# Hybrid decoder trunk: the forget sums' transfer to DRAM is issued by ScalarE's queue instead of SP's

## The chip, the core and the metric

The kernel runs on one core of a Trainium2 chip. A core has five engines, each with its own queue of instructions: TensorE (PE, with its weight loads as PEld), VectorE (DVE), ScalarE (ACT), GpSimd (POOL) and SyncE (SP), which computes nothing and issues transfers. They wait for each other through semaphores. The metric is the device time of one execution in microseconds; of several runs the median is taken.

## What is computed

Two layers of a decoder trunk over 528 tokens (16 learned meta tokens and 512 real ones) of width 1024, in float32. In each layer a normalised input goes through one input projection; half of its columns feed eight heads of forgetting attention, half feed four heads of retention; their outputs go through one output projection and are added; then a SwiGLU feed-forward with 2816 hidden columns follows. At the end the tokens are normalised and the meta tokens are dropped.

The part that the change touches is the decay of the forgetting attention. Eight columns of the projection are forget gates, one per head:

```
logf = log_sigmoid(flog + b_fgate)
c    = cumsum(logf, axis=1)
s    = q k^T * scale + c[t] - c[s],  s <= t
p    = softmax(s)
```

The running sum c is needed along the keys, that is, as one row of 528 numbers per head which every query's partition must see. Within a row of the softmax, c[t] is a constant and falls out, so that the kernel only uses the part over the keys.

## The kernel before

All activations lie transposed, channels on the 128 partitions and the 528 tokens along the row. Every float32 product is made of three products of split numbers: a high part (a cast) and a low part (the difference), for weights and activations; so a weight tile of 128x1024 is loaded by SP into one of three `raw` buffers (`fetch`, L158), cast in two halves by ScalarE into `whi` (L191), subtracted by GpSimd or VectorE into `wlo` (L194), and then used by TensorE (L217). The load of a tile waits in SP's queue until an earlier tile's splitting has set its buffer free.

The order of TensorE's work is written out by hand: `layer` builds lists of steps (projections, attention heads, retention heads) and merges them by places, so that the steps of the heads stand between those of the projections. The order on the other engines is made by a scheduler that takes the instructions' priorities and dependences; only the instructions that are pinned keep the program's order. A transfer stands in the queue of the engine that issues it, at the place which the scheduler gives it there, and a queue is worked off in order.

The piece around the change, once per layer:

- `forget_gates` (L367) multiplies the normalised input by the gates' weights and leaves the eight gates as rows of 528 in `z`.
- `forget_sums` (L389) scales them, takes the log-sigmoid with ScalarE (L394 to L396) and VectorE (L397, L398), and sums along the row by a scan (L399). The result, 8 partitions by 528, 16.5 KB, is written to a tensor in DRAM, `cdr` (L401).
- `scores` (L492) of each head reads its row of `cdr` back into all 128 partitions, a tile `bc` of 264 KB, two buffers (L497, issued by SP). Then for each block of queries TensorE makes the scores (L507), VectorE adds the mask (L513) and subtracts `bc` while taking the row's minimum (L514), and ScalarE takes the exponential (L527).

```
        nc.vector.tensor_tensor_scan(z2, z, z, 0.0, ALU.add, ALU.max)
        st["cdr"] = tc.dram_tile([FH, T], F32, name=f"cdr{l}")
        nc.sync.dma_start(st["cdr"], z2)
...
                nc.sync.dma_start(bc, ly["cdr"][hd:hd + 1, :].partition_broadcast(128))
```

Other names that are used below: `kh` and `kl` are the split keys of the head pair (L451, L452), `vt` the transposed values (L458 and L627), `vv` the split values after TensorE's transposes (L418, L483, L484). PSUM tiles are `psa` (four buffers, scores and transposes) and `psd` (two buffers, projections): a step that needs a `psa` buffer waits until the reader of its last use is done.

Of the kernel before, what the change touches and what calls it, by code (L numbers as in the profile page):

```python
# [39 lines left out]
def hybrid_kernel(ctx, tc, x_t, w_in, w_fl, w_out, w_gate, w_up, w_down, vecs, b_fg, rope, decay, mask, ident, out_t):  # L40
    nc = tc.nc
# [224 lines left out]
    def tt(name, dt=F32):  # L266
        tag, bufs = tags[name]
        return tmp.tile([128, T], dt, name=name, tag=tag, bufs=bufs)
# [120 lines left out]
    def forget_sums(l, st):  # L389
        z = st["z"]  # L390
        z2 = tt("z2")[0:FH]
        with ExitStack() if l else tc.high_priority():
            nc.vector.scalar_tensor_tensor(z, z, RSC, st["R"][0:FH, :], ALU.mult, ALU.mult)
            nc.scalar.activation(z2, z, AF.Abs, bias=bfg[:, l:l + 1])  # L394
            nc.scalar.activation(z2, z2, AF.Exp, scale=-1.0)
            nc.scalar.activation(z2, z2, AF.Ln, bias=onec[0:FH])  # L396
        nc.vector.tensor_scalar(z, z, bfg[:, l:l + 1], 0.0, ALU.add, ALU.min)  # L397
        nc.vector.tensor_sub(z, z2, z)  # L398
        nc.vector.tensor_tensor_scan(z2, z, z, 0.0, ALU.add, ALU.max)  # L399
        st["cdr"] = tc.dram_tile([FH, T], F32, name=f"cdr{l}")  # L400
        nc.sync.dma_start(st["cdr"], z2)  # L401

    LOGS = "natural_log_exp_and_others"
    ROOTS = "abs_reciprocal_sqrt_and_small"
# [821 lines left out]
    def layer(l):  # L1226
# [62 lines left out]
        def first_parts():  # L1289
            ly["parts"] = col_parts(ly["acc"], FULL, True)  # L1290
            convert(3, NK, True)

        sums = [lambda: forget_sums(l, ly)]
        plan = [lambda: enter_att(l), start]
        if l == 0:
# [109 lines left out]
```

## Time and profile before

| what | value |
|---|---|
| time, median of 3 runs | 1274.46 us (1274.37 to 1275.15) |
| the profiled execution's own time | 1278.19 us |
| its span, first to last instruction | 1276.3 us |
| mean granted TensorE clock | 0.995 |
| busy share: PE, PEld, DVE, ACT, POOL | 99%, 94%, 78%, 54%, 21% |
| transfers by SP's queue (q1) | 118.77 MB, 29.8% of 16 engines' span |
| transfers by ScalarE's queue (q10) | 0.29 MB |
| cdr to DRAM, issued by SP | twice, at 36.0 and 672.0 us |

Times in the profile are microseconds from the span's start. The profile's rows give start and length, the engine, the line of the kernel, the operation, and the output and input tiles; a count follows the x. In brackets stand the engine's idle time just before the row and what ended it. SPq and ACTq mark what SP's and ScalarE's sequencers do themselves: issuing transfers and waiting. The chain of waits is followed back from the last instruction: at each step to what released it. A row of it that begins with DMA lasts from the issue to the moment at which the waiting engine went on.

### The profile page before, as it was taken

How to read it: one execution, taken by the hardware profiler on the slowest of the kernel's cores; microseconds unless marked ns; L12 is line 12 of the kernel's file. 1: busy time of each engine (PE TensorE's matmuls, PEld its weight loads, DVE VectorE, ACT ScalarE, POOL GpSimd, SP SyncE). 2: the span in 40 equal slices, each digit the busy share in tenths (PEclk: the TensorE clock that was granted, in tenths of full speed). 3: DMA queues.
4: the chain of work that ended last, by engine and by line, in shares of the span. 5: the costliest groups of instructions: out<-in, count | busy, mean ns of one | idle time of the engine just before them, and what ended most of it. 6: DMA issues, size and time to landing. Idle time of an engine off the chain costs nothing.

```text
span 1276.3 us, 23615 instructions
## 1 busy us (share of the span) xinstructions
PE 1258.8 (99%) x9271; PEld 1199.9 (94%) x9271; DVE 996.6 (78%) x1843; ACT 688.2 (54%) x1246; POOL 265.2 (21%) x522
## 2 busy tenths in 40 slices
PE   9999999999999999999999999999999999999997
PEld 8899999999999999999998989999789999999996
DVE  7777856779988887887785777567899888888866
ACT  6666545676444444444464665456764444444444
POOL 3355546420000000000025545554100000000000
PEclk9999999999999999999999999999999999999998
DMA  6322232223333333332323232232224333333321
GB/s 216 93 68 84 79 94 72 74 67 112 108 96 100 100 100 100 100 100 83 102 74 100 76 100 84 75 92 67 99 86 129 100 100 100 100 99 101 106 76 67
DMA packets 45680, 120.57 MB, mean 94 GB/s; under 512 B 5360, under 2 KB 12272, under 8 KB 45568
## 3 DMA queue, kind: packets, MB, share of 16 engines
q1 hardware_dynamic: 45136, 118.77, 29.8%
q8 instruction: 73, 1.20, 0.4%
q14 instruction: 39, 0.32, 0.1%
q10 hardware_dynamic: 432, 0.29, 0.1%
HBM read 116.91 MB, written 2.13 MB: 93 GB/s over the span
## 4 chain that ended last, share of the span: by engine, by line
PE 94%; DVE 2%; ACT 1%; DMA 1%; issue 0%; DVEq 0%; ACTq 0%; SPq 0%
PE psd L217 30%; PE psa L880 18%; PE psd L1015 14%; PE psd L880 13%; PE psa L217 5%; PE psa L1015 4%; PE psa L418 2%; PE psa L572 2%; PE psa L507 2%; PE psa L729 1%; PE psa L699 1%; DMA bc<-cdr 1%; PE psa L379 1%; PE psa L290 0%; DMA cdr<-z 0%
## 5 line engine op out<-in xcount | busy, mean ns | idle before, releaser
L194 POOL TENSOR_TENSOR wlo<-raw,whi 128x128 fp32r<-128x128 f32 x504 | 259.9, 551 | 293.5 <-ACT whi L191 293.5
L217 PE MATMUL psd<-xh,whi 128*128 128x264 f32 (+1 forms) x792 | 197.1, 316 | 0.6 <-ACT whi L191 0.6
L217 PE MATMUL psd<-xh,wlo 128*128 128x264 f32 (+1 forms) x792 | 187.7, 305 | 0.0
L217 PE MATMUL psd<-xl,whi 128*128 128x264 f32 (+1 forms) x792 | 187.3, 304 | 0.4 <-DVE xl L320 0.4
L217 PEld LDWEIGHTS psd<-xh,whi 128*128 128x128 f32 x792 | 129.4, 191 | 5.7 <-ACT whi L191 1.3
L217 PEld LDWEIGHTS psd<-xh,wlo 128*128 128x128 f32 x792 | 128.0, 190 | 6.4 <-DVE wlo L194 0.4
L217 PEld LDWEIGHTS psd<-xl,whi 128*128 128x128 f32 x792 | 128.6, 190 | 4.8 <-DVE xl L320 0.8
L191 ACT CAST whi<-raw 128x512 fp32r<-128x512 f32 (+1 forms) x168 | 98.5, 614 | 51.6 <-PE psd L217 38.2
L868 ACT CAST whi<-raw 128x1024 fp32r<-128x1024 f32 (+2 forms) x62 | 54.9, 886 | 51.0 <-PE psd L880 39.5
L868 ACT CAST fwhi<-raw 128x1024 fp32r<-128x1024 f32 (+2 forms) x62 | 55.7, 898 | 46.6 <-PE psd L880 39.2
L1115 POOL TENSOR_TENSOR th<-th,e 128x544 f32<-128x544 f32 x1 | 1.4, 1370 | 359.1 <-DVE e L1135 359.1
L85 POOL MEMSET kl<- 64x528 f32 x2 | 1.1, 534 | 345.4 <-PE psa L880 345.4
L869 DVE TENSOR_TENSOR wlo<-raw,whi 128x1024 fp32r<-128x1024 f32 (+2 forms) x62 | 62.9, 1015 | 12.1 <-ACT whi L868 12.0
L869 DVE TENSOR_TENSOR fwlo<-raw,fwhi 128x1024 fp32r<-128x1024 f32 (+2 forms) x62 | 64.0, 1032 | 9.6 <-ACT fwhi L868 9.5
L880 PE MATMUL psa<-th,whi 128*128 128x264 f32 (+1 forms) x232 | 65.4, 282 | 0.0
L880 PE MATMUL psa<-th,wlo 128*128 128x264 f32 (+1 forms) x232 | 65.4, 282 | 0.0
L880 PE MATMUL psa<-tl,whi 128*128 128x264 f32 (+1 forms) x232 | 65.3, 282 | 0.0
L880 PE MATMUL psa<-th,fwhi 128*128 128x264 f32 (+1 forms) x224 | 63.4, 283 | 0.0
L880 PE MATMUL psa<-tl,fwhi 128*128 128x264 f32 (+1 forms) x224 | 63.3, 283 | 0.0
L880 PE MATMUL psa<-th,fwlo 128*128 128x264 f32 (+1 forms) x224 | 63.2, 282 | 0.0
L527 ACT ACTIVATE probs<-probs,nmax 128x144 f32<-128x144 f32 (+1 forms) x64 | 36.9, 577 | 47.3 <-DVE nmax L514 34.5
L868 ACT CAST fwhi<-S 128x1024 fp32r<-128x1024 f32 x20 | 21.0, 1050 | 69.1 <-PE psa L880 67.1
(340 smaller groups left out, 4053.7 us busy)
## 6 DMA issues: line engine op xcount, KB each, us to landing
raw<-w_in SPq DMA_DIRECT2D x54, 512.0 KB, 3.5
raw<-w_gate SPq DMA_DIRECT2D x44, 512.0 KB, 3.8
fraw<-w_up SPq DMA_DIRECT2D x38, 512.0 KB, 3.5
raw<-w_down SPq DMA_DIRECT2D x64, 256.0 KB, 2.8
raw<-w_out SPq DMA_DIRECT2D x16, 512.0 KB, 3.4
raw<-w_down SPq DMA_DIRECT2D x32, 192.0 KB, 2.5
bc<-cdr SPq DMA_DIRECT2D x16, 264.0 KB, 3.4
raw<-w_up SPq DMA_DIRECT2D x6, 512.0 KB, 3.6
```

Source lines behind the costliest of these rows:

```text
L191: pin(nc.scalar.copy(hi, job["raw"][:, c0:c1]), pinned)
L194: pin(sub(lo[:, i:i + step], job["raw"][:, c0 + i:c0 + i + step], hi[:, i:i + step].bitcast(F32)), pinned)
L217: nc.tensor.matmul(ps[1][b][:, 0:c1 - c0], w[:, wk, :], x[:, c0:c1], start=(k == 0 and i == 0), stop=(k == n - 1 and i == 2))
L379: nc.tensor.matmul(ps[:, 0:c1 - c0], wf[:, k, :], st["x"][k][part][:, c0:c1], start=(i == 0), stop=(i == 2 * NK - 1))
L418: nc.tensor.transpose(ps[:, 128 * j:128 * j + 128], src[:, o:o + 128], idt)
L507: nc.tensor.matmul(sc[0:nq, 0:c1 - c0], st["q"][s][:, q0:q0 + nq], kk[:, c0:c1], start=(i == 0), stop=(i == 1))
L527: nc.scalar.activation(pr, pr, AF.Exp, bias=nmax[0:nq], scale=-1.0, accum_out=rsum)
L572: nc.tensor.matmul(po[:, c0:SEQ], v[:, j, :], pp[:, j, META + c0:T], start=(j == 0 and i == 0), stop=(j == 4 and i == 1))
L868: nc.scalar.copy(hi, src)
L869: nc.vector.tensor_sub(lo, src, hi.bitcast(F32))
L880: nc.tensor.matmul(bank()[:, 0:b.shape[-1]], a[:, o + k, :], b, start=(fresh and k == 0 and i == 0), stop=(k == n - 1 and i == 2), skip_gr ...
L1015: nc.tensor.matmul(v[:, 0:c1 - c0], a[:, s * n + k, :], b[:, c0:c1], start=(k == 0 and i == 0), stop=(k == n - 1 and i == 2))
```

## The change

`forget_sums` hands its transfer to ScalarE's queue. Nothing else in the text of the kernel is touched.

```
         nc.vector.tensor_sub(z, z2, z)
         nc.vector.tensor_tensor_scan(z2, z, z, 0.0, ALU.add, ALU.max)
         st["cdr"] = tc.dram_tile([FH, T], F32, name=f"cdr{l}")
-        nc.sync.dma_start(st["cdr"], z2)
+        nc.scalar.dma_start(st["cdr"], z2)
```

What this does to the order of the queues, in layer 1 first. SP's queue after the loads of the angles (`cr`, `sr`), before the change:

```order
L1237 DMA cr<-rope 128x528
L1237 DMA sr<-rope 128x528
L158 DMA raw<-w_in 128x1024
L679 DMA dec<-decay 128x528
L158 DMA raw<-w_in 128x1024 x2
L401 DMA cdr_8605<-z_8597 8x528
L497 DMA bc<-cdr_8605 128x528 x2
L158 DMA raw<-w_in 128x1024 x2
```

Now the L401 is gone, and the two reads of `cdr` stand right behind the two weight loads. It stands in ScalarE's queue instead, which reads now, from the log-sigmoid to the first exponential of the attention:

```order
L394 ACTIVATE z_8597<-z,bfg 8x528
L395 ACTIVATE z_8597<-z_8597 8x528
L396 ACTIVATE z_8597<-z_8597,onec 8x528
L191 CAST whi<-raw 128x512 x2
L451 CAST kh_8672<-tq 64x528 x2
L401 DMA cdr_8605<-z_8597 8x528
L451 CAST kh_8676<-tq 64x528 x2
L191 CAST whi<-raw 128x512 x3
L527 ACTIVATE probs,sums<-probs,nmax 128x144
```

Before, the same rows stood there without the L401.

In layer 0 the transfer comes behind all four casts of the keys on ScalarE, and one cast of the values (`vv_603`) moves up ahead of the first exponentials:

```order
 L451 CAST kh_428<-tq 64x528 x2
 L451 CAST kh_432<-tq 64x528 x2
+L401 DMA cdr_424<-z_414 8x528
 L191 CAST whi<-raw 128x512 x2
 L483 CAST vv_602<-psa 128x4x64
 L483 CAST vv_602<-psa 128x64
+L483 CAST vv_603<-psa 128x4x64
 L527 ACTIVATE pm_113,rsum<-pm_113,nmax 16x16
 L527 ACTIVATE probs,sums<-probs,nmax 128x144
-L483 CAST vv_603<-psa 128x4x64
```

VectorE's order in layer 0 follows this: the first subtraction of the values (L484) now stands ahead of the first step that reads `bc` (L514).

```order
 L627 SCALAR_TENSOR_TENSOR vt_108<-psd,R 128x528
 L513 TENSOR_TENSOR psa<-psa,msk 128x128
+L484 TENSOR_TENSOR vv_602<-psa,vv_602 128x4x64
 L514 ISA pm_113,nmax<-psa,bc 16x16
 L514 ISA nmax 16x1
 L514 ISA probs,nmax<-psa,bc 128x144
 L514 ISA nmax 128x1
-L484 TENSOR_TENSOR vv_602<-psa,vv_602 128x4x64
```

Behind these rows five more subtractions, masks and L514 steps of the same blocks change places with each other. The order on TensorE and GpSimd is the same as before, and so is VectorE's in layer 1.

More of the change, by code (lines that the diff above doesn't have):

```diff
@@ L400, in forget_sums @@
         st["cdr"] = tc.dram_tile([FH, T], F32, name=f"cdr{l}")
-        nc.sync.dma_start(st["cdr"], z2)
+        nc.scalar.dma_start(st["cdr"], z2)
     LOGS = "natural_log_exp_and_others"
```

## The prediction

> **What bounds the kernel now.** I read the page first, then the waits of TensorE, then the chain of waits in layer 1, and last the timelines of the queues around it.
>
> ```profile
> span 1276.3 us, 23615 instructions
> PE 1258.8 (99%) x9271; PEld 1199.9 (94%) x9271; DVE 996.6 (78%) x1843; ACT 688.2 (54%) x1246; POOL 265.2 (21%) x522
> ```
>
> TensorE is the bound; a change pays only if it shortens one of its few stalls. These are the waits in which it took part near the two transfers that are moved (engine and line, what ended the wait, total, times, longest):
>
> ```profile
> PE psa L418 <- DVE vv L484: 1.8, 1, 1.8
> PE psa L507 <- DVE nmax L514: 1.1, 1, 1.1
> PE psa L418 <- DVE nmax L514: 0.6, 1, 0.6
> ```
>
> The 1.8 and the 0.6 stand in layer 1, the 1.1 in layer 0. What leads to those of layer 1 is told by the chain of waits from 660 to 690 us (start, length, what):
>
> ```profile
> 671.60 0.33 SPq L158
> ...
> 671.98 3.25 DMA cdr<-z
> ...
> 675.24 3.90 DMA bc<-cdr
> ...
> 679.28 0.31 DVE probs L514
> ...
> 683.42 0.41 PE psa L418
> ```
>
> The forget sums go to DRAM (cdr) and come back broadcast (bc), and the first scores step of the attention waits for bc. That round trip is on the path. Was it started as soon as it could be? The timelines of VectorE and SP, and a stage row (stretch, length, busy us of PE, PEld, DVE, ACT, POOL, the granted clock, DMA share, GB/s) answer:
>
> ```profile
> 666.25 1.40 DVE L399 TENSOR_TENSOR_SCAN z<-z 8x528 f32<-8x528 f32 x1
> 659.27 12.66 SPq L158 DMA_DIRECT2D raw<-w_in  x2
> 662.90:671.60 8.70, 8.70 (x75) 8.70 (x74) 5.68 (x9) 6.72 (x11) 5.52 (x9) 1.00 0.00 1
> ```
>
> The scan ends at 667.65. SP issues cdr only at 671.98, 4.33 us later: it stands in SP's queue behind a weight load that waits for its buffer until 671.60, while the DMA engines lie idle (share 0.00). And cdr then takes 3.25 us, since it travels behind 512 KB of weights.
>
> **What the change removes and adds.** Two issues leave SP and join ScalarE, one per layer; the bytes are the same. In layer 0 VectorE's and ScalarE's orders shift a little too.
>
> When does ScalarE issue? In its queue cdr stands behind casts (kh), and behind it stand the other casts. Whether the issue waits for the casts ahead to finish is shown by how far its sequencer runs ahead (instruction, count, ns min/median/max, first and last start; ACTq is the sequencer):
>
> ```profile
> L191 ACTq EVENT_SEMAPHORE  x1: 4291/4291/4291, 665.2 to 665.2; - x1
> 666.43 2.60 ACT L451 CAST kh<-tq 64x528 fp32r<-64x528 f32 x4
> L191 ACTq EVENT_SEMAPHORE  x1: 3550/3550/3550, 33.9 to 33.9; - x1
> 33.84 2.60 ACT L451 CAST kh<-tq 64x528 fp32r<-64x528 f32 x4 [0.47 <-DVE tq L444]
> ```
>
> The wait behind the four casts began at 665.2 and at 33.9, when the casts had hardly begun: the sequencer had handed them over. So cdr needs only the scan.
>
> *Layer 1, the round trip.* Issue at 667.68 (scan end 667.65 plus about 0.03). In layer 0, with nothing ahead in the queue, the same transfer took 1.47 (row below), so it is in DRAM at about 669.2. SP goes on being held until 671.60, issues its weight load (0.33), and then bc at 671.98, in cdr's old place, without a wait: 3.26 earlier than 675.24. When does bc land? It now rides directly behind 512 KB of weights, which before cdr did. Nearest rows: the pair took 3.90 in the chain above; a later bc, issued 0.43 after a weight load, landed 3.6 after its issue:
>
> ```profile
> 806.41 0.33 SPq L158 DMA_DIRECT2D raw<-w_in  x1
> 806.84 0.38 SPq L497 DMA_DIRECT2D bc<-cdr  x1
> DMA to landing us min/median/max: 3.6/3.6/3.6
> raw<-w_in SPq DMA_DIRECT2D x54, 512.0 KB, 3.5
> ```
>
> That is 675.6 to 675.9 against 679.15. I take 675.9. The bound on the other side is no overlap at all: the weights land 3.5 after 671.60 (their median, last row), then 3.90: 679.0.
>
> *Layer 1, TensorE.* Its rows around the stall, then the same work at full pace, and the granted clock:
>
> ```profile
> 679.85 0.34 PE L507 MATMUL psa<-kh,qs 128*128 128x400 f32 x1
> 680.03 0.34 PE L507 MATMUL psa<-kl,qs 128*128 128x400 f32 x1
> 680.96 0.66 PE L418 MATMUL psa<-idt,vt 128*128 128x128 f32 x4 [0.58 <-DVE nmax L514]
> 683.42 0.41 PE L418 MATMUL psa<-idt,vt 128*128 128x128 f32 x1 [1.80 <-DVE vv L484]
> ...
> 686.99 0.40 PE L217 MATMUL psd<-xh,whi 128*128 128x512 f32 x1
> 677.20 0.40 PE L217 MATMUL psd<-xh,whi 128*128 128x512 f32 x1
> 677.90 0.71 PE L418 MATMUL psa<-idt,vt 128*128 128x128 f32 x5
> 678.37 0.48 PE L217 MATMUL psd<-xh,whi 128*128 128x512 f32 x1
> 62.94 0.49 PE psa L507 x4
> 683.40:687.00 3.60, 3.58 (x12) 3.08 (x13) 3.01 (x11) 0.72 (x2) 0.00 (x0) 0.53 0.44 146
> ```
>
> TensorE could have gone on at 680.21 (680.03 plus the 0.18 from 679.85 to 680.03). From there to 686.99 it does five transposes, three psd matmuls, four L507 matmuls and three psd matmuls. At full pace that is 0.47 (677.90 to 678.37) + 0.70 (677.20 to 677.90) + 0.49 + 0.70 = 2.36, so 682.57. It took until 686.99: 4.42 us lost. From 683.42 to 686.99 alone one transpose (0.09) and 1.89 of matmuls took 3.57, so 1.59 of the loss is the clock, granted at 0.53 after the stalls. The other 2.83 is standing still.
>
> How early must bc be for the loss to vanish? Both stalls end a fixed chain after bc (679.15): the first at 680.96, 1.8 after it; the second at 683.42, 4.27 after it. TensorE comes to them at 680.21 and, four transposes later, at about 680.6. So bc must land by 678.4 for the first and by 676.3 for the second. 675.9 meets both, with 0.4 to spare on the second. Gain: **4.42**.
>
> The Trainium skill, "TensorE: Matmul & The Clock Gate" (Part 1: The HAM clock gate), says the clock falls to half after an idle window of about 3.4 us. Here it fell after 0.58 and 1.80 us of idling with transposes between, shorter than that window. By the rule alone the 1.59 would not be there and the sum would be 2.83; I go by the row.
>
> *Layer 1, what stands behind.* On ScalarE the last two kh casts start some 0.3 later (an issue holds the sequencer 0.33 on SP), at 668.0; the subtraction that reads them ends before 669.6, when VectorE waits 0.48 for TensorE:
>
> ```profile
> 669.62 0.77 DVE L458 SCALAR_TENSOR_TENSOR vt<-psa,R 128x264 f32<-128x264 f32 x2 [0.48 <-PE psa L217]
> ```
>
> So nothing; without that cover, 0.3 at most. SP's next weight load stood behind the bc pair and comes earlier by at most as much as bc; it rides behind bc, not ahead of it.
>
> *Layer 0.* Here SP was not held up (chain of waits, then VectorE and TensorE):
>
> ```profile
> 34.70 1.23 DVE L399 TENSOR_TENSOR_SCAN z<-z 8x528 f32<-8x528 f32 x1
> 35.96 1.47 DMA cdr<-z
> 37.45 3.84 DMA bc<-cdr
> 41.43 0.16 DVE L514 CUSTOM_DVE_ANT_0 pm<-psa,bc 16x16 f32<-16x16 f32 x1 [2.18 <-DMA bc<-cdr]
> 41.66 0.39 PE L507 MATMUL psa<-kh,qs 128*128 128x272 f32 x1 [1.09 <-DVE nmax L514]
> ```
>
> The scan ends at 35.93; from ScalarE's sequencer the issue is again at about 35.96. The next wait on ScalarE lasts to 37.4, which hides the issue itself. If the issue had to wait for the four casts (end 36.44), the round trip and TensorE's 1.09 would grow by 0.49. Bounds: 0 and 0.49 lost; no gain is possible, since cdr already left with the scan's end. I take 0, by the two sequencer rows. The subtraction L484 that now stands ahead of L514 on VectorE runs in the 2.18 that VectorE waits for bc, so the L514 that ends TensorE's wait does not move; if L484 came too late it would push L514 by its own length, well under that wait, and I take nothing for it.
>
> *Afterwards.* Does TensorE keep the 4.4?
>
> ```profile
> 700.00:1200.00 500.00, 499.61 (x3269) 454.96 (x3268) 399.14 (x701) 272.84 (x476) 105.04 (x208) 1.00 0.31 95
> ```
>
> From 700 to 1200 us it is busy 499.61 of 500, so work that comes earlier ends earlier. Sum: 1274.46 - 4.42 - 0 = **1270.0 us**. The profiled execution took 1278.19 with its span of 1276.3, 3.7 above the median of the runs; the difference of two executions is carried over to that median.
>
> **The rivals.**
>
> *The clock term is missing in unprofiled runs.* The stall stays, its aftermath doesn't, because the fall of the clock after so short a stall is chance: for it, the 1.09 in layer 0 left no half-clock stretch; against it, one row shows it. Then 1274.46 - 2.83 = 1271.6.
>
> *The queue of weights keeps bc.* cdr is early, but bc now waits behind the 512 KB itself and lands near 679.0: gain 0.15, so 1274.3. For it: cdr needed 3.25 there against 1.47. Against it: the 3.6 of the bc at 806.84. It decides from a landing after 678.4 (nothing left but part of the second stall). The Trainium skill, "DMA: Bandwidth & Descriptors" (Issuing engines are not separate DMA queues), says that a second issuing engine saves only the sequencer's issue time; that speaks for this rival. The idle 8.7 us show that here it is a wait, not an issue, that is spared.
>
> *Given back.* TensorE runs 4.4 ahead of the weights' splitting, and stalls on POOL's slow halves:
>
> ```profile
> 692.82 2.64 POOL L194 TENSOR_TENSOR wlo<-raw,whi 128x128 fp32r<-128x128 f32 x4 [2.10 <-ACT whi L191]
> ```
>
> These wait on ScalarE, which follows the round trip and moves by 3.26, about 1.2 less than TensorE. If that were all stall: 1271.2; with a second one of that kind or a fall of the clock, 1273.
>
> *Slower: ScalarE's own DMA queue is slow.* Its only earlier weights took 4.8 to land:
>
> ```profile
> raw<-w_in ACTq DMA_DIRECT2D x2, 128.0 KB, 4.8
> ```
>
> Were cdr to take 4.8, bc in layer 0 would start 3.3 later, TensorE would stand 4.4 and then run 1.59 longer at half clock: 4.9 lost, against 4.4 won in layer 1 (cdr landed at 672.5, bc 2.8 earlier): 1275.0. From 4.3 on the change loses. Against it: those loads went out beside all of the start's traffic, cdr alone.
>
> That ScalarE's issue waits for casts would not undo the change: 0.49, so 1270.5. That is inside the forecast.
>
> **How the numbers follow.** Forecast 62%, the missing clock term 13%, weights keep bc 11%, given back 7%, slow queue 7%. 0.2% is 2.55 us, about what the runs can tell apart. Faster by more: 62, 10 of the 13 (1271.6 lies 0.3 inside the bound) and 3 of the 7: 75%. Slower by more: 5 of the last 7. Within: 20%. Range: down to 1269.2 (the gain plus 0.3 in layer 0 and the spread of the runs), up to 1272.8, which takes in the first two cases and most of the fourth.
>
> **What would show it.** cdr issued near 667.7 and bc near 672.0 in layer 1; bc landed by 676.3; no wait at L418 after it and a clock of 1.00 where 0.53 stood; in layer 0 cdr still at 36.0 and the 1.09 unchanged. A bc landed after 678, a longer stall at L507 in layer 0, or a new wait of TensorE on L194 would each make the forecast wrong.

## The result and the profile after

| | before | after |
|---|---|---|
| median of 12 runs each, side by side | 1274.87 us (1273.77 to 1277.92) | 1272.55 us (1271.73 to 1273.09) |
| ratio after/before, 95% interval | | 0.9975 [0.9967, 0.9983] |
| profiled execution, own time (span) | 1278.19 us (1276.3) | 1272.86 us (1271.1) |
| mean granted clock in it | 0.995 | 0.997 |

The kernel is faster by a quarter of a per cent: 0.0025 of 1274.87 is 3.2 us, with the interval 2.2 to 4.2. The medians lie 2.3 apart (their ratio is 0.9982, which the interval takes in), the means of the 12 runs 2.9 (1275.46 and 1272.54), the two profiled executions 5.33. Why these differ is the question that the experiments had to settle.

First the queues in layer 1, from the timelines of VectorE, ScalarE and SP of the changed kernel (start, length, engine, line, what; the idle time ahead in brackets):

```profile
665.88 1.40 DVE L399 TENSOR_TENSOR_SCAN z<-z 8x528 f32<-8x528 f32 x1
...
666.05 1.28 ACT L451 CAST kh<-tq 64x528 fp32r<-64x528 f32 x2
667.31 0.28 ACTq L401 DMA_DIRECT2D cdr<-z  x1
667.63 1.29 ACT L451 CAST kh<-tq 64x528 fp32r<-64x528 f32 x2 [0.30 <-DVE z L399]
...
658.90 12.65 SPq L158 DMA_DIRECT2D raw<-w_in  x2
671.60 0.90 SPq L497 DMA_DIRECT2D bc<-cdr  x2
...
675.86 0.31 DVE L514 CUSTOM_DVE_ANT_0 probs<-psa,bc 128x144 f32<-128x144 f32 x1 [0.90 <-DMA bc<-cdr]
```

cdr leaves at 667.31, 0.03 behind the scan's end (667.28) and 4.67 us earlier than before (671.98). SP is held by the same weight load up to 671.55, and then bc goes out where cdr stood. VectorE's first step that needs bc starts at 675.86; before it was 679.28. The two casts behind the issue waited 0.30.

TensorE's rows at the place of the two stalls, and a stage row over 674 to 684 us of the kernel before and of the changed one (stretch, length, busy us of PE, PEld, DVE, ACT, POOL, clock, DMA share, GB/s). Before:

```profile
674.00:684.00 10.00, 7.61 (x45) 6.31 (x44) 3.57 (x13) 3.23 (x10) 4.33 (x11) 0.97 0.42 136
```

After:

```profile
679.29 0.39 PE L217 MATMUL psd<-xh,wlo 128*128 128x512 f32 x1
...
679.70 0.34 PE L507 MATMUL psa<-kl,qs 128*128 128x400 f32 x1
679.88 0.71 PE L418 MATMUL psa<-idt,vt 128*128 128x128 f32 x5
680.34 0.48 PE L217 MATMUL psd<-xh,whi 128*128 128x512 f32 x1
...
683.59 0.41 PE L217 MATMUL psd<-xh,wlo 128*128 128x264 f32 x2
...
674.00:684.00 10.00, 10.00 (x63) 8.81 (x62) 6.54 (x24) 4.87 (x14) 4.16 (x11) 1.00 0.47 164
```

The five transposes run as one group, without a wait, and TensorE is busy for the whole 10 us at full clock. How much was won there is read from one VectorE step on either side of the place. Ahead of it is L458: 669.62 before (shown in the prediction) and 669.30 after. Behind it is L143, before and then after:

```profile
688.97 1.43 DVE L143 TENSOR_TENSOR rvl<-sq,rvh 128x512 fp32r<-128x512 f32 x2 [1.31 <-ACT rvh L142]
```

```profile
669.30 0.77 DVE L458 SCALAR_TENSOR_TENSOR vt<-psa,R 128x264 f32<-128x264 f32 x2
...
684.26 1.42 DVE L143 TENSOR_TENSOR rvl<-sq,rvh 128x512 fp32r<-128x512 f32 x2 [0.57 <-ACT rvh L142]
```

The lead is 0.32 ahead of the place and 4.71 behind it: 4.39 us were won in between, in this pair of executions. At the end the lead is 5.2 (spans of 1276.3 and 1271.1), so nothing of it was given back.

### The profile page after: what moved, and what is told of

Read it like the earlier page. It is cut to its first block, busy times and chain, and to the rows that moved or that the text cites. A ratio compares the mean times of both kernels' runs of the same rounds, so it can differ in the third digit from the quotient of the medians.

```text
span 1271.1 us, 23615 instructions
## 1 busy us (share of the span) xinstructions
PE 1256.1 (99%) x9271; PEld 1197.9 (94%) x9271; DVE 996.9 (78%) x1843; ACT 687.2 (54%) x1246; POOL 264.9 (21%) x522
## 4 chain that ended last, share of the span: by engine, by line
PE 92%; DVE 4%; ACT 2%; DMA 1%; issue 1%; ACTq 0%; DVEq 0%
PE psd L217 29%; PE psa L880 18%; PE psd L1015 14%; PE psd L880 13%; PE psa L217 5%; PE psa L1015 4%; PE psa L418 2%; PE psa L572 2%; PE psa L507 2%; PE psa L729 1%; PE psa L699 1%; PE psa L379 1%; DMA raw<-w_in 0%; ACT whi L191 0%; PE psa L290 0%
## 5 line engine op out<-in xcount | busy, mean ns | idle before, releaser
L946 ACT COPY e<-psa 128x264 f32<-128x264 f32 (+1 forms) x114 | 42.8, 375 | 28.4 <-PE psa L880 24.1
```

The costliest lines, as they stand in the source:

```text
L946: nc.scalar.copy(self.t["e"][:, i], self.t["x"][:, 0:w])
```

## The experiments

The theory: what is won is the standing still of TensorE in layer 1, because bc lands earlier, because cdr no longer waits in SP's queue; the half clock behind the stall is extra and not always there. Rivals: the gain needs ScalarE's own queue; or it comes from layer 0 or from the orders that moved along with it.

**How sure is the comparison?** The kernel before, against itself. 

> The kernel before against itself; nothing is changed. Open is why the runs moved by 2.3 us in the median (ratio 0.9975) where the two profiles moved by 5.2. Theory 'two kinds of execution': some executions of the kernel before contain the stretch at half clock after the layer-1 stall (the profile did), others only the stall. Then the runs fall into two groups, one near 1274.5 with a mean granted clock near 0.997 and a smaller one near 1277 with a clock near 0.995, and the ratio is 1.000. Rival 'the profile stretches transfers': then the runs form one group near 1274.5 with one clock, and only a profiled execution is long.

Measured: ratio 0.9998 [0.9989, 1.0007]; 1275.58 us (1273.67 to 1276.87). The comparison shows no bias. But the kernel before spreads, in two groups: of its 59 runs beside the experiments, these eleven included, 26 lie between 1273.18 and 1274.79 (mean 1274.2), 32 between 1275.44 and 1278.16 (mean 1276.4), and one at 1275.08; both groups stand on each of the two chips that the experiments ran on. A run's mean granted clock is 0.997 to 0.999 in the first group and 0.995 to 0.997 in the second. So there are two kinds of execution, but the long kind is not the rarer one. The rival falls, since many runs besides the profiled ones are long. Twenty runs of the changed kernel, here and below, lie between 1270.94 and 1273.09 (mean 1272.4). Part of the spread of before is therefore something that the change removes. This execution of the kernel before, one of the long group, shows what that can be (TensorE, and the stage row):

```profile
678.54 0.66 PE L418 MATMUL psa<-idt,vt 128*128 128x128 f32 x4 [0.31 <-DVE nmax L514]
681.00 0.30 PE L418 MATMUL psa<-idt,vt 128*128 128x128 f32 x1 [1.80 <-DVE vv L484]
681.53 0.63 PE L217 MATMUL psd<-xl,whi 128*128 128x512 f32 x1
...
680.00:684.00 4.00, 3.00 (x10) 2.65 (x11) 3.21 (x12) 1.21 (x4) 0.00 (x0) 0.65 0.41 131
```

The same two stalls, 0.31 and 1.80, and again a fallen clock behind them (0.65 over four us, a 512-column matmul at 0.63 in place of 0.39 to 0.40).

**Layer 1 alone, and layer 0 alone.** The transfer is moved in one layer and left with SP in the other:

```
-        nc.scalar.dma_start(st["cdr"], z2)
+        (nc.scalar if l else nc.sync).dma_start(st["cdr"], z2)     # layer 1 alone
+        (nc.sync if l else nc.scalar).dma_start(st["cdr"], z2)     # layer 0 alone
```

> ScalarE issues cdr in layer 1, SP in layer 0. By my reading layer 1 is the whole of the gain: ratio as with the full change, 0.9975 (within 0.0008), bc issued right behind the weight load in layer 1, no wait of TensorE at L418 there, layer 0 as before. Rival 'part of the gain comes from layer 0' (the profile of the change shows TensorE 0.5 us sooner past the first bc there): then at least 0.4 us of it is missing, ratio 0.9979 or above.

> ScalarE issues cdr in layer 0, SP in layer 1. By my reading no gain: ratio 1.000 (0.9993 to 1.0007), cdr issued with the scan's end as before, and all of the layer-1 stall still there (cdr held 4.3 us behind the scan's end, 3.3 us to land). Rival 'part of the gain comes from layer 0': ratio 0.9996 or below, by 0.5 us.

Measured: layer 1 alone 1271.2 us (1271.14 to 1272.42), ratio 0.9968 [0.9956, 0.9980]; layer 0 alone 1274.52 us (1273.43 to 1277.0), ratio 0.9997 [0.9988, 1.0006]. In the kernel with layer 1 alone, the orders of TensorE, VectorE, ScalarE's computing and GpSimd are those of before, so the shifts in layer 0 aren't needed. Layer 1 is the whole gain, as far as these intervals tell. The kernel with layer 0 alone has TensorE's stall still, but in the profiled execution without the half clock (TensorE, and the stage row):

```profile
678.32 0.35 PE L507 MATMUL psa<-kl,qs 128*128 128x400 f32 x1
678.79 0.66 PE L418 MATMUL psa<-idt,vt 128*128 128x128 f32 x4
681.25 0.30 PE L418 MATMUL psa<-idt,vt 128*128 128x128 f32 x1 [1.80 <-DVE vv L484]
681.62 0.39 PE L217 MATMUL psd<-xl,whi 128*128 128x512 f32 x1
...
680.00:684.00 4.00, 2.75 (x16) 2.36 (x16) 3.66 (x14) 1.21 (x4) 0.25 (x1) 1.00 0.46 131
```

The stall of 1.80 is the same as in the rows above. The first one is shorter: the transposes start 0.47 behind the last L507 matmul (678.32), against 0.93 in the prediction's rows (680.03 to 680.96). The clock stays at 1.00. So the half clock follows the stalls in some executions and not in others.

**The place in the queue, or the other queue?** cdr stays with SP in both layers; in layer 1 cdr is kept ahead of two weight loads, so that it doesn't wait for a weight buffer. The first bc moves up with it, and every other engine keeps its order:

```
-        nc.scalar.dma_start(st["cdr"], z2)
+        pin(nc.sync.dma_start(st["cdr"], z2), l)
...
-        return sum([dense_steps(w_in[l, base + job[c][0]], [...], True)
+        return sum([dense_steps(w_in[l, base + job[c][0]], [...], True, late_load=l and hd == 0 and c == "k")
```

(`late_load` pins that one projection's weight load, so that it stays behind cdr; the second load follows it.)

> cdr stays in SP's queue in both layers, but in layer 1 it is kept ahead of two weight loads that stood before it; bc of the first head moves up with it. If the gain is the place in a queue (nothing held ahead of cdr), this wins as much as the change without ScalarE: cdr issued at the scan's end, about 0.03 behind it, landed 1.5 us later, bc landed some 5.5 us after the scan's end, no wait of TensorE at L418 in layer 1, ratio 0.9975 (0.9967 to 0.9983). The weight loads behind it come up to 10 us later than before but are needed only some 6 us after that, so no new wait on L194 or L191. Rival 'a second queue is what helps, since its transfers run beside those of SP': then ratio 0.999 to 1.000, or slower, as SP is now held by the scan and the weights come late.

Measured: 1272.15 us (1270.73 to 1273.4), ratio 0.9972 [0.9962, 0.9982]. SP's timeline and a stage row:

```profile
665.65 0.29 SPq L401 DMA_DIRECT2D cdr<-z  x1
667.13 0.34 SPq L497 DMA_DIRECT2D bc<-cdr  x1
667.58 2.31 SPq L158 DMA_DIRECT2D raw<-w_in  x2
...
674.00:688.00 14.00, 14.00 (x97) 12.89 (x96) 11.18 (x36) 9.10 (x27) 7.20 (x15) 1.00 0.30 96
```

With SP as the issuer the same gain comes, and cdr is in DRAM 1.48 after its issue (667.13), as in layer 0. The queue of ScalarE is not needed; what counts is that cdr doesn't stand behind a load that waits. bc is issued at 667.13; this execution runs 1.62 ahead of that of the changed kernel (cdr of layer 0 at 34.30 and 35.92), so bc goes out 2.9 us earlier still than there (671.60), and this brings nothing more: once the stall is gone, no one waits for an earlier bc.

**The changed kernel and layer 1 alone again, on one chip.** No edit but those above.

> The changed kernel itself, again, on the same chip as the three runs that follow. Theory (the standing still in layer 1, 2.83 us, is what the change wins always; the half clock behind it, 1.59 us, stood only in a part of the executions of the kernel before): ratio 0.9975, between 0.9966 and 0.9980, and its times lie closer together than those of the kernel before, since the stall that sometimes halved the clock is gone. Rival (the half clock followed the stall always and the change costs about 1 us elsewhere): the same ratio, but the times of the kernel before lie as close together as those of the changed one.

> Only layer 1's transfer on ScalarE's queue, again, beside the changed kernel on one chip. Theory (layer 1 is the whole gain, layer 0 is worth nothing): ratio within 0.0007 of the changed kernel's. Rival (issuing from ScalarE costs 1 us in layer 0, as 0.9968 against 0.9975 would say): ratio lower by 0.0007 to 0.001 again.

Measured: 1272.49 us (1270.94 to 1272.95), ratio 0.9973 [0.9963, 0.9983], and 1271.85 us (1271.15 to 1272.99), ratio 0.9973 [0.9963, 0.9984]. The two ratios are equal, so the 0.0007 between them in the first comparison was no cost of layer 0. The changed kernel's eight times lie within 2.0 us, those of the kernel before on this chip within 4.1, as the theory has it and the rival doesn't.

**Is it bc's landing? Delay it.** The changed kernel, with one or three extra reads of `cdr` ahead of layer 1's first bc, into spare tiles:

```
-                nc.sync.dma_start(bc, ly["cdr"][hd:hd + 1, :].partition_broadcast(128))
+                [pin(nc.sync.dma_start(d, ly["cdr"][hd:hd + 1, :].partition_broadcast(128)), ly["l"])
+                 for d in [at(f"bcx{i}", F32, bufs=1)
+                           for i in range(N if (ly["l"], g, s) == (1, 0, 0) else 0)] + [bc]]
```

N is 1 or 3, `ly["l"]` the number of the layer. The orders of TensorE, VectorE, ScalarE and GpSimd are those of the changed kernel; in SP's queue some later weight loads and reads change places.

> The changed kernel, with the first broadcast of layer 1 read twice: once into a spare tile that nobody reads, then into its own. It delays bc and nothing that computes. Theory (only bc's landing counts: no loss up to 676.3, the second stall from there, both from 678.4): 264 KB more cost between 1.0 and 1.9 us, so bc lands at 676.7 to 677.6 instead of 675.73; TensorE waits 0.4 to 1.3 us at L418 and not before it; ratio 0.9978 to 0.9986 against the kernel before, 0.3 to 1.0 us behind the changed kernel. Rival (the gain comes with another thing that moved along with cdr, and bc's landing has some 3 us to spare): no wait, ratio as the changed kernel's, 0.9975.

> The changed kernel, with the first broadcast of layer 1 read four times, the first three into spare tiles that nobody reads. Theory: bc lands 3.0 to 5.7 us later, at 678.7 to 681.4, around or behind where the kernel before had it (679.15); both stalls are back, 2.83 us moved by as much as bc is earlier or later than 679.15, so 2.4 to 5.1 us of standing, and the half clock returns in a part of the executions; ratio 0.9993 to 1.0020, and the times spread as those of the kernel before. Rival (the gain comes with another thing that moved along with cdr): ratio stays below 0.9985.

Measured: read twice 1273.26 us (1272.67 to 1274.32), ratio 0.9983 [0.9974, 0.9992]; read four times 1279.84 us (1279.02 to 1281.09), ratio 1.0034 [1.0021, 1.0046]. Read twice, the chain of waits and TensorE's rows:

```profile
671.35 4.86 DMA bc<-cdr
...
679.09 0.60 PE L418 MATMUL psa<-idt,vt 128*128 128x128 f32 x4
680.48 0.30 PE L418 MATMUL psa<-idt,vt 128*128 128x128 f32 x1 [0.79 <-DVE vv L484]
680.86 0.40 PE L217 MATMUL psd<-xl,whi 128*128 128x512 f32 x1
```

bc lands at 676.21. This execution runs 0.73 ahead of the changed kernel's (first read issued at 670.87 and 671.60), so on that one's clock bc lands at 676.94, as expected (676.7 to 677.6). TensorE's second stall ends 4.27 us after the landing, at 680.48: the fixed chain of the prediction. The first stall isn't there, the second is back with 0.79, the clock does not fall (0.40), and the median is 0.77 behind the changed kernel's. Read four times:

```profile
672.51 8.20 DMA bc<-cdr
...
678.78 0.40 PE L217 MATMUL psd<-xh,wlo 128*128 128x512 f32 x1
681.22 0.45 PE L507 MATMUL psa<-kh,qs 128*128 128x400 f32 x1 [2.04 <-DVE nmax L514]
682.53 0.66 PE L418 MATMUL psa<-idt,vt 128*128 128x128 f32 x4 [0.68 <-DVE nmax L514]
684.98 0.45 PE L418 MATMUL psa<-idt,vt 128*128 128x128 f32 x1 [1.80 <-DVE vv L484]
...
690.93 0.40 PE L217 MATMUL psd<-xh,wlo 128*128 128x264 f32 x2
...
684.00:690.00 6.00, 5.02 (x15) 4.07 (x16) 4.28 (x16) 1.31 (x5) 0.00 (x0) 0.50 0.25 88
```

bc lands at 680.71, again 4.27 ahead of the end of the last stall.

The waits in brackets sum to 2.04 + 0.68 + 1.80 = 4.52 (before: 2.38). Counted as the prediction counted its 2.83, the standing still is more: from the last psd matmul to the fifth transpose 6.20 pass (678.78 to 684.98), in the changed kernel 0.96 (679.29 to about 680.25), so 5.24, just above the 2.4 to 5.1 expected. From there to the same later matmul it takes 5.95 (to 690.93) against 3.34 (to 683.59): 2.61 more, with the clock at 0.50 for the whole stretch from 684 to 690 us, longer than the 3.6 us before. Together that is 7.85, of the 8.20 between the two profiled executions and beside the 7.35 between the medians.

So the ratio is outside what was expected (0.9993 to 1.0020). All six runs lie within 2.1 us of each other, where a spread as that of the kernel before was expected: after the longer stall the half clock seems to come always, which six runs and one profile don't prove. The rival that bc's landing has room to spare falls.

## Why the prediction was right, and where its size was off

**What bounds, and the place** (right). The stall hung on cdr's 4.33 us behind a waiting weight load: layer 1 alone gives the whole ratio, and putting cdr ahead within SP's own queue gives it too.

**ScalarE issues at the scan's end** (right). In layer 1 the run can't tell, because the scan and the two casts ahead of the issue ended within 0.05 us of each other. In layer 0 it can (ScalarE's timeline of the changed kernel):

```profile
33.80 2.61 ACT L451 CAST kh<-tq 64x528 fp32r<-64x528 f32 x4 [0.48 <-DVE tq L444]
35.92 0.53 ACTq L401 DMA_DIRECT2D cdr<-z  x1
```

The issue was made at 35.92, while the four casts still ran to 36.41. The prediction's row for layer 1 says more than was read from it: the wait behind the casts began at 665.2, before the first of them (666.43).

**bc's landing** (right). Predicted: issue 671.98, landing 675.9, bound 679.0. Measured: issue 671.60, and VectorE starts on it at 675.86, 0.13 after its landing as in the chain before (3.90 from 675.24 gave 679.15, the step 679.28), so 675.73, 4.13 after the issue. The rival that the weights keep bc to 679 fell with this: read in the same way, bc took 3.91 to 4.18 in the four profiles of the changed kernel and of layer 1 alone, with the weights ahead of it, and 3.18 to 3.90 in the three with the stall of before, so the weights cost it at most about 1 us, not 3.5.

**When TensorE needs bc** (right). The two limits, 676.3 and 678.4, held: 675.73 leaves no wait (by the changed kernel's own rows the fifth transpose comes at about 680.25, and 4.27 ahead of that is 675.98, so 0.25 was to spare, not 0.4), and the two delays put the stalls back in the predicted order and with the predicted chain of 4.27.

**Layer 0** (right in effect). The prediction took nothing, and layer 0 alone measures 0.9997. In the profiled pair the wait at L507 did go from 1.09 to 0.56, where the prediction had called a gain impossible, because bc took less time (VectorE and TensorE of the changed kernel):

```profile
37.43 0.81 SPq L497 DMA_DIRECT2D bc<-cdr  x2
...
40.86 0.16 DVE L514 CUSTOM_DVE_ANT_0 pm<-psa,bc 16x16 f32<-16x16 f32 x1 [0.32 <-DMA bc<-cdr]
...
41.09 0.39 PE L507 MATMUL psa<-kh,qs 128*128 128x272 f32 x1 [0.56 <-DVE nmax L514]
```

That step came 3.43 after the issue of bc, against 3.98 before (37.45 to 41.43). The change does not explain it: with layer 0's transfer left with SP, the same wait was 0.5 in the kernel before against itself and 0.7 in layer 1 alone, the second time. The 1.09 is the largest of the ten profiles (the others 0.45 to 0.65), so the wait differs from execution to execution.

**The sum: the term that was mis-sized.** The step that failed is "the difference of two executions is carried over to that median". The 4.42 was right for the execution it was read from: 4.39 were won there. But that execution, 3.7 above the median, was one in which the half clock followed the stall, and of the runs behind the median of 1274.46 (1274.37 to 1275.15) two lie in the short group and none in the long one. The 1.59 of the half clock is paid by a part of the executions. What every execution pays is nearer the 2.83 of standing still: counted in the same way it is 2.56 in the kernel before against itself and 2.37 with layer 0 alone. The groups of runs say the same: the short one lies 1.8 above the changed kernel's mean, the long one 4.0, and the two are about equally large, so the mean gain stands between, and a median of few runs falls on either side. That the long group is the one with the half clock is not shown run by run. Three profiled executions with these stalls fit it (1278.19 and 1275.62 with the half clock, 1273.71 without), and so do the groups' mean clocks, but a run's mean clock alone doesn't tell: the changed kernel's profile has 0.997 without a stall.

The rival "the clock term is missing", put at 13%, gave 1271.6, a ratio of 0.9978; the forecast of 1270.0 is 0.9965; measured were 0.9975 and 0.9973, nearer the rival. The median of 1272.55 lies only 0.25 below the upper end of the range: it fell inside because the range made room for this rival, not because the sum was right.

How much one execution varies can be taken apart with the profiles at hand. Subtracting from each profiled execution's own time the moment at which cdr was issued in layer 0 takes out the start of the kernel:

| kernel | own time | cdr of layer 0 | difference | stalls in layer 1 | clock behind them |
|---|---|---|---|---|---|
| before | 1278.19 | 35.96 | 1242.23 | 0.58 + 1.80 | 0.53 |
| before, against itself | 1275.62 | 34.16 | 1241.46 | 0.31 + 1.80 | 0.65 |
| layer 0 alone | 1273.71 | 34.52 | 1239.19 | 1.80 and a short one | 1.00 |
| changed, read twice | 1273.13 | 35.14 | 1237.99 | 0.79 | 1.00 |
| changed | 1272.86 | 35.92 | 1236.94 | none | 1.00 |
| changed, again | 1272.17 | 35.41 | 1236.76 | none | 1.00 |
| layer 1 alone | 1271.14 | 34.46 | 1236.68 | none | 1.00 |
| layer 1 alone, again | 1272.99 | 35.97 | 1237.02 | none | 1.00 |
| cdr ahead in SP's queue | 1271.32 | 34.30 | 1237.02 | none | 1.00 |
| changed, read four times | 1280.37 | 35.34 | 1245.03 | 2.04 + 0.68 + 1.80 | 0.50 |

The five executions without a stall agree within 0.4 us. The stalls of before cost 2.3 more without the half clock, and 4.6 to 5.3 with it (0.5 of the 5.3 is that execution's longer wait in layer 0). By these profiles, few as they are, the gain of the change has two sizes, by execution. So the figures of the result differ: the profiled pair (5.33) sets a long execution against the changed kernel, the medians (2.3) rest on twelve runs before of which six are short and four long, and the means (2.9) mix them all.

**Kept afterwards, given back, a slow queue of ScalarE** (right to keep, rightly given low chances). The lead grew from 4.71 to 5.2 behind layer 1's place. cdr from ScalarE took 1.51 in layer 0 (35.92 to bc's issue at 37.43), not 4.8.

## What to carry to other kernels

Look in a queue for a transfer whose data is ready and that stands behind one which waits for a buffer: the time it is held is read from the producer's end to the issue row, and a move to any place where nothing waits, in another engine's queue or further up in the same one, can win it, as far as something waits for the data. Work out from the consumer's side when the data is needed, since an arrival before that moment is worth nothing: here some 3 us earlier took the whole gain, and another 2.9 brought no more. A gain that is read off one execution belongs to that execution; where part of it follows from the clock, compare its time with the spread of the runs before adding that part to their median.

## What the runs showed that I had not expected

The fall of the clock after a stall of TensorE is not a fixed price: behind 1.80 us it was missing once, though a short stall went ahead of it; behind 0.31 + 1.80 and 0.58 + 1.80 it lasted some 3.5 us, and behind 2.04 + 0.68 + 1.80 it lasted nearly 7. Three profiled executions with the shorter stalls are too few to say what decides.

The start of the kernel varies too, by up to 1.8 us, and shows in every later time. Two neighbouring pairs of matmuls of the first projection, in the profiled execution of the kernel before, against itself, and then in its first profile:

```profile
6.34 0.41 PE L217 MATMUL psd<-xl,whi 128*128 128x264 f32 x2
6.59 0.41 PE L217 MATMUL psd<-xh,wlo 128*128 128x264 f32 x2
```

```profile
8.39 0.64 PE L217 MATMUL psd<-xh,whi 128*128 128x264 f32 x2
8.83 0.64 PE L217 MATMUL psd<-xl,whi 128*128 128x264 f32 x2
```

The pairs follow each other by 0.25 us in the one and by 0.44 in the other, there until 10.6 us. This is no effect of the change: one and the same kernel has cdr of layer 0 early and late (the kernel before at 34.16 and 35.96, layer 1 alone at 34.46 and 35.97). It may go with the chip, since the four profiles taken on one chip have it at 34.16 to 34.52 and the four on another at 35.14 to 35.97. The pace of these pairs doesn't explain all of it: the kernels with bc read twice and four times have the fast pairs and cdr at 35.14 and 35.34. Its cause stays open.
